# The values of an attention head, taken later inside the gate projection, with the low part of P last

## The chip, the cores and the metric

One NeuronCore of one Trainium2 chip. The metric is the device time of one execution in microseconds; lower is better. The kernel before takes 2942.22 us (median of 3 runs, 2941.56 to 2946.38).

## The reference, cut to what matters

Two layers of a decoder trunk on one sequence of 256 positions, width 2048, in f32. Each layer computes a normalised input `u`, one wide projection of it, an attention branch and a gated linear recurrence side by side, merges them with two sigmoid gates, and then runs an MLP and a per-layer embedding step.

```python
cq_raw, ckv_raw, xb, yb, gate_a, gate_r = split_columns(u @ w_in[l])
...
pr = jax.nn.softmax(sc, axis=-1).astype(v.dtype)
outs.append(jnp.einsum('bhqk,bkhd->bqhd', pr, v[:, :s1]))
...
merged = jax.nn.sigmoid(gate_a) * attn + jax.nn.sigmoid(gate_r) * rec
x = x + merged @ w_out[l]
```

The change is about the second line of the attention, probabilities (P) times values, for 16 heads with causal masking in two blocks of 128 queries.

## The kernel before, in words

**Arithmetic.** Every f32 operand of a matmul is split into a high and a low part (`hi` and `lo`, both of the type that TensorE takes), and a product is three matmuls: high by high, high by low, low by high (`mm3`, lines 214 to 219). ScalarE makes the high part (line 122 for weights, 964 for P), VectorE subtracts to get the low part (lines 126 and 967).

**Weights.** They arrive as blocks of 128 x 1024 ("halves" in the code, called blocks here), 1004 in all, by one DMA queue, into six raw buffers. `half()` (lines 202 to 212) starts the use of block h: it first splits block h + 2 (`split_half`, lines 117 to 128, three buffers each for `hi` and `lo`, so the new `hi` waits for the use of block h - 1 to end), and then lets the planner issue other work. `mm_half` (221 to 229) then issues the 24 matmuls of the block: 8 slices of 128 rows, three matmuls each, 256 columns wide.

**The planner.** The order of ScalarE's and VectorE's queues is written at build time by a small simulation. `E` holds a clock for each engine (P is TensorE); work is a list of jobs with steps, each step an engine, a cost and a function; jobs of lower rank come first. `later` adds a job, `need` makes TensorE's clock wait for one (and issues it if it was not yet), `work` issues the steps that start before a limit for each engine, those with no idle time first. `work` runs only inside `half()`: once between the `hi` and the `lo` of the split, with the limit for VectorE 0.18 below ScalarE's clock and none of ScalarE's own steps, and once after the split, with limits of P + 3.5 for VectorE and P + 2.6 for ScalarE. These are the lines that set it:

```python
        A.activation(hi, src, AF.Copy)
        E["A"] = max(E["A"], E["P"]) + 0.95
        work(E["A"] + LATENCY - 0.3, E["A"])
        V.tensor_tensor(out=lo, in0=src, in1=f(hi), op=ALU.subtract)
        E["V"] = max(E["V"], E["A"] + LATENCY) + 1.14
```

A product of one slice costs P 0.328, LATENCY is 0.12, and a step that follows another of its job starts 0.12 after it on another engine or the same.

**A group.** A layer's mixer runs 8 groups of two heads. For each group TensorE projects, in this order, the recurrence's input (`xb`, 4 blocks), its gelu branch (`yb`, 4), keys, values, queries and rope queries (1 each), the recurrence gate (`gr`, 4) and the attention gate (`ga`, 4); in group 0 `gr` comes ahead of the keys. Attention is threaded between those blocks by hooks, functions that `mm_pair` (line 250) and, for the last group's gate, `mm_apart` (line 261) call at the end of a block. In groups 1 to 7 the hooks of `gr` are `early` (line 992: scores of head 0 after block 2, of head 1 after block 3) and those of `ga` are `late`: after block 0 the transposes of head 0's P (`turned(0)`, line 955), after block 1 the values of head 0 and the transposes of head 1 (`values0`, 987), after block 2 the values of head 1 (`values(1)`, 971). In group 0 `early` sits in `ga`, and `late` in the `xb` blocks of group 1.

`turned` adds a job of rank -2 with two steps: the high part on ScalarE into `PT[0]` (line 964) and the low part on VectorE into `PT[1]` (line 967). `values` waits for it, takes the one bank of tag `o`, which must have been emptied of the head before (the copy `oT`, line 983, a job of rank -1), and issues six matmuls: for the first 128 keys, 256 columns (all queries), and then for the second 128 keys, 128 columns, each time high V by high P, high V by low P, low V by high P.

**The recurrence** is a job of rank 1 (line 906) whose last steps fall into the gate's blocks: `rec_b` (lines 894 to 896, planner cost 1.0), `rec_c`, a product and a scan (899 and 901, cost 1.3), `rec_d` (904, cost 0.6); then a job `recg` (782, cost 0.6).

Of the kernel before, what the change touches and what calls it, by code (L numbers as in the profile page):

```python
# [18 lines left out]
P = 128  # L19
S = 256  # L20
# [56 lines left out]
def trunk_kernel(ctx: ExitStack, tc: tile.TileContext, xT, pT, pos, par, gfin, invf, wu, out):  # L77
# [13 lines left out]
    V, A, T, G = nc.vector, nc.scalar, nc.tensor, nc.gpsimd  # L91

    def f(ap):
        return ap.bitcast(F32)
# [19 lines left out]
    E = {"P": 0.0, "V": 0.0, "A": 0.0, "G": 0.0}  # L114
# [55 lines left out]
    def later(key, *steps, deps=(), rank=1, also=()):  # L170

        job = Job((key, *also), rank, deps, steps)
        at = len(jobs)
        while at and jobs[at - 1].rank > rank:
            at -= 1
        jobs.insert(at, job)

    def need(key):

        if key not in done:  # L180
            next(j for j in jobs if key in j.keys).force()
        E["P"] = max(E["P"], done[key] + LATENCY)
# [19 lines left out]
    def half():  # L202
        h = nxt["used"]
        nxt["used"] += 1
        while nxt["half"] <= min(h + min(LA, max(h - 1, 0)), n_halves - 1):
            split_half(nxt["half"])
            nxt["half"] += 1
        load_to(h + PD)
        work(E["P"] + WINDOW + 0.9, E["P"] + WINDOW)
        hi, lo, at = halves.pop(h)  # L210
        E["P"] = max(E["P"], at)
        return hi, lo

    def mm3(o, wh, wl, ah, al, start, stop, shared=False):

        T.matmul(o, lhsT=wh, rhs=ah, start=start, stop=False, skip_group_check=shared)  # L216
        T.matmul(o, lhsT=wh, rhs=al, start=False, stop=False, skip_group_check=shared)  # L217
        T.matmul(o, lhsT=wl, rhs=ah, start=False, stop=stop, skip_group_check=shared)  # L218
        E["P"] += 0.328

    def mm_half(o, act, s, first=True, shared=False):


        hi, lo = half()
        for kk in range(8):
            k = 8 * s + kk
            need((act[1], k))
            c = slice(kk * P, (kk + 1) * P)
            mm3(o, hi[:, c], lo[:, c], act[0][:, k, 0, :], act[0][:, k, 1, :], first and k == 0, k == 15, shared)

    readers = {}

    def bank(tag, name, key):

        pool, bufs = banks[tag]
        last = readers.setdefault(tag, [])
        if len(last) >= bufs:
            need(last[-bufs])
        last.append(key)
        return pool.tile([P, 512], F32, tag=tag, name=name)  # L240

    def mm_bank(name, key):
        return bank("mm", name, key)

    def mm_tile(ps, act):

        for i in range(2):
            mm_half(ps[:, 0:S], act, i)

    def mm_pair(name, key, act, hooks=(), crossed=False):  # L250


        ps = mm_bank(name, key)
        for i in range(4):
            t, s = (i % 2, i // 2) if crossed else (i // 2, i % 2)
            mm_half(ps[:, t * S:(t + 1) * S], act, s, t == 0, True)
            if i < len(hooks) and hooks[i] is not None:
                hooks[i]()
        return ps

    def mm_apart(name, keys, act, hooks=()):

        for t in range(2):
            ps = mm_bank(f"{name}_{t}", keys[t])
            for s in range(2):
                mm_half(ps[:, 0:S], act, s)
                i = 2 * t + s
                if i < len(hooks) and hooks[i] is not None and s == 0:
                    hooks[i]()
            yield t, ps[:, 0:S]  # L270
            if i < len(hooks) and hooks[i] is not None:
                hooks[i]()

    def dup(r, n=2):
        return r.unsqueeze(1).to_broadcast([P, n, S])
# [4 lines left out]
    def t512(name):  # L280
        return tmp.tile([P, 512], F32, tag="t", name=name)
# [345 lines left out]
    def mixer(l, u, mg, norm):  # L627
# [73 lines left out]
        for g in range(GROUPS):  # L701
            first = group(l, g, u, mg, norm, cn, kr, first, rot_kr if g == 0 else None)

    def group(l, g, u, mg, norm, cn, kr, first, rot_kr):
# [3 lines left out]
        t_ = {}  # L708


        ps_x = mm_pair(f"xb_{nm}", ("xb", nm), u, first)

        def xb():
# [24 lines left out]


        ps_y = mm_pair(f"yb_{nm}", ("yb", nm), u)  # L740

        def y_evac():
# [62 lines left out]
        hi, lo = half()  # L805
        ps_v = mm_bank(f"v_{nm}", ("v", nm))
        for j in range(2):
            o = ps_v[:, j * S:(j + 1) * S]
# [49 lines left out]
        for t in range(2):  # L858
            ps_l = bank("s", f"lru{t}_{nm}", ("lru", t, nm))
            sl = slice(t * S, (t + 1) * S)  # L860
            for w in range(2):
                c = slice(512 + (2 * w + t) * P, 512 + (2 * w + t + 1) * P)
# [49 lines left out]
        def scores(t):  # L912
            for k in (("k", nm), ("q", nm), ("rot", f"q{nm}"), ("rot", f"k{l}")):
                need(k)
            s = bank("s", f"s{t}_{nm}", ("p", t, nm))
            for j in (1, 0):

                n = (j + 1) * P
                o = s[:, (1 - j) * S:(1 - j) * S + n]
                q = [t_["q"][w][:, t * S + j * P:t * S + (j + 1) * P] for w in "hl"]  # L920
                kk = [t_["k"][w][:, t * S:t * S + n] for w in "hl"]
                mm3(o, q[0], q[1], kk[0], kk[1], True, False)

                qr = t_["qr"]["q"][t][:, j * P:(j + 1) * P]
                for m, w in enumerate("hl"):
                    T.matmul(o, lhsT=qr, rhs=kr["rot"][w][:, 0:n], start=False, stop=m == 1)
                E["P"] += 0.22

            cols = (slice(0, S), slice(S, S + P))
            w = {}  # L930

            def mask_max():
                w["sm"] = t512(f"sm{t}_{nm}")
                w["st"] = tiny.tile([P, 8], F32, tag="st", name=f"st{t}_{nm}")
                for n, c in enumerate(cols):
                    V.tensor_tensor_reduce(
                        out=w["sm"][:, c], in0=s[:, c], in1=mask[:, n * P:S], scale=1.0, scalar=-3.0e38,
                        op0=ALU.add, op1=ALU.max, accum_out=w["st"][:, n:n + 1],
                    )
                V.tensor_scalar(out=w["st"][:, 2:4], in0=w["st"][:, 0:2], scalar1=-SCALE, scalar2=None, op0=ALU.mult)  # L940

            def expo():
                e = t_["p", t] = att.tile([P, 384], F32, tag=f"p{t}", name=f"p{t}_{nm}")
                for n, c in enumerate(cols):
                    A.activation(e[:, c], w["sm"][:, c], AF.Exp, bias=w["st"][:, 2 + n:3 + n], scale=SCALE, accum_out=w["st"][:, 4 + n:5 + n])

            def scale():
                V.reciprocal(w["st"][:, 6:8], w["st"][:, 4:6])
                e = t_["p", t]
                for n, c in enumerate(cols):  # L950
                    V.tensor_scalar(out=e[:, c], in0=e[:, c], scalar1=w["st"][:, 6 + n:7 + n], scalar2=None, op0=ALU.mult)

            later(("p", t, nm), ("V", 0.75, mask_max), ("A", 0.65, expo), ("V", 0.5, scale), rank=-1)

        def turned(t):
            need(("p", t, nm))
            e = t_["p", t]
            pt = bank("t", f"pt{t}_{nm}", ("pt", t, nm))
            T.transpose(pt[:, 256:384], e[:, 256:384], ident)
            T.transpose(pt[:, 384:512], e[:, 0:128], ident)  # L960
            T.transpose(pt[:, 128:256], e[:, 128:256], ident)

            def high():
                A.activation(PT[0][:, P:512], pt[:, P:512], AF.Copy)

            def low():
                V.tensor_tensor(out=PT[1][:, P:512], in0=pt[:, P:512], in1=f(PT[0][:, P:512]), op=ALU.subtract)

            later(("pt", t, nm), ("A", 0.4, high), ("V", 0.5, low), rank=-2)

        def values(t):
            need(("pt", t, nm))
            need(("v", nm))
            o = bank("o", f"o{t}_{nm}", ("o", t, nm))
            h, lo = PT
            for j, c in ((0, slice(S, 512)), (1, slice(P, S))):
                cc = slice(j * S + t * P, j * S + (t + 1) * P)
                mm3(o[:, j * P:S], t_["v"]["h"][:, cc], t_["v"]["l"][:, cc], h[:, c], lo[:, c], j == 0, j == 1)

            def evac():  # L980
                if t == 0:
                    t_["oT"] = att.tile([P, 512], F32, tag="oT", name=f"oT_{nm}")
                A.activation(t_["oT"][:, t * S:(t + 1) * S], o[:, 0:S], AF.Copy)

            later(("o", t, nm), ("A", 0.27, evac), rank=-1)

        def values0():
            values(0)
            turned(1)


        early, late = (None, None, lambda: scores(0), lambda: scores(1)), (lambda: turned(0), values0, lambda: values(1))
        if g:
            rec_gate(early)
        def merge_steps(t0, n):
# [21 lines left out]
        hooks = late if g else early  # L1017
# [349 lines left out]
```

## Time and profile before

| | |
|---|---|
| median of 3 runs | 2942.22 us |
| the profiled execution's own time | 2949.3 us |
| its span, first to last instruction | 2947.5 us |
| granted TensorE clock, mean | 0.998 |
| TensorE busy (matmuls) | 2907.9 us, 99% |
| VectorE busy | 1864.3 us, 63% |
| ScalarE busy | 1538.9 us, 52% |

TensorE executes 24800 matmuls, almost all of 128 x 128 by 256 columns. A matmul row is about 0.28 us long because it is pipelined; how fast TensorE goes is seen in the distance between starts. PE is TensorE, PEld its weight loads, DVE VectorE, ACT ScalarE. In a timeline a row gives the start, the duration, the engine, the line, the operation and the tiles (written from read), and in brackets the idle time of the engine just before it and what ended it.

### The profile page before, as it was taken

The page shows a single profiled execution, that of the slowest core. Times are in us where ns is not written, and L with a number is a line of the kernel's source. Part 1 is how long each engine was busy: PE and PEld are TensorE (multiplying, and loading weights), DVE is VectorE, ACT ScalarE, POOL GpSimd, SP SyncE. Part 2 cuts the span into 40 slices and gives each one's busy share as a digit, 9 for nine tenths or more (in the row PEclk, how much of TensorE's full clock was granted, in tenths as well). Part 3 has the DMA queues.
Part 4 walks back from the last instruction along what each step waited for, and adds up shares of the span by engine and source line. Part 5 has one row for each costly group of instructions (what it writes and reads, how often), then busy time and mean ns, then how long its engine had stood idle before and what let it go on. Part 6 is the DMA issues. An engine that isn't in the chain of part 4 may idle for free.

```text
span 2947.5 us, 58412 instructions
## 1 busy us (share of the span) xinstructions
PE 2907.9 (99%) x24800; PEld 2896.9 (98%) x24800; DVE 1864.3 (63%) x2420; ACT 1538.9 (52%) x2050; POOL 8.9 (0%) x17
## 2 busy tenths in 40 slices
PE   8999999999999999999999999999999999999998
PEld 8999999999999999999999999999999999999998
DVE  7877777765555454556758777776654555555565
ACT  5666666644344343444546666666543444434445
POOL 0000000000000000000000000000000000000000
PEclk9999999999999999999999999999999999999999
DMA  7555455555555555555555555555555555555553
GB/s 238 168 173 178 165 170 175 172 186 186 186 187 186 186 187 187 191 186 190 190 185 171 173 166 166 174 176 177 189 187 187 186 187 187 188 188 190 186 186 129
DMA packets 146998, 535.23 MB, mean 182 GB/s; under 512 B 16560, under 2 KB 16816, under 8 KB 146736
## 3 DMA queue, kind: packets, MB, share of 16 engines
q1 hardware_dynamic: 146736, 531.50, 54.9%
q8 instruction: 194, 3.18, 0.4%
q14 instruction: 68, 0.56, 0.0%
HBM read 529.33 MB, written 2.10 MB: 180 GB/s over the span
## 4 chain that ended last, share of the span: by engine, by line
PE 93%; DVE 3%; ACT 3%; issue 1%; DMA 0%; ACTq 0%; SPq 0%; POOLq 0%
PE down L218 8%; PE up L218 8%; PE down L217 8%; PE down L216 8%; PE up L216 8%; PE up L217 8%; PE yb L217 2%; PE gr L216 2%; PE yb L218 2%; PE yb L216 2%; PE out L217 2%; PE gr L218 2%; PE out L218 2%; PE gr L217 2%; PE out L216 2%; PE pg L217 2%
## 5 line engine op out<-in xcount | busy, mean ns | idle before, releaser
L126 DVE TENSOR_TENSOR lo<-raw,hi 128x1024 fp32r<-128x1024 f32 x1004 | 1229.8, 1225 | 878.5 <-ACT hi L122 876.3
L122 ACT ACTIVATE hi<-raw 128x1024 fp32r<-128x1024 f32 x1004 | 1066.0, 1062 | 1376.3 <-PE down L217 411.5
L216 PE MATMUL up<-bufA,hi 128*128 128x256 f32 x1024 | 287.9, 281 | 0.0
L216 PE MATMUL down<-bufB,hi 128*128 128x256 f32 x1024 | 287.7, 281 | 0.0
L217 PE MATMUL down<-bufB,hi 128*128 128x256 f32 x1024 | 287.7, 281 | 0.0
L218 PE MATMUL down<-bufB,lo 128*128 128x256 f32 x1024 | 287.7, 281 | 0.0
L216 PE MATMUL down<-bufA,hi 128*128 128x256 f32 x1024 | 287.7, 281 | 0.0
L217 PE MATMUL down<-bufA,hi 128*128 128x256 f32 x1024 | 287.7, 281 | 0.0
L218 PE MATMUL down<-bufA,lo 128*128 128x256 f32 x1024 | 287.7, 281 | 0.0
L216 PE MATMUL up<-bufB,hi 128*128 128x256 f32 x1024 | 287.7, 281 | 0.0
L217 PE MATMUL up<-bufA,hi 128*128 128x256 f32 x1024 | 287.6, 281 | 0.0
L218 PE MATMUL up<-bufA,lo 128*128 128x256 f32 x1024 | 287.6, 281 | 0.0
L218 PE MATMUL up<-bufB,lo 128*128 128x256 f32 x1024 | 287.5, 281 | 0.0
L217 PE MATMUL up<-bufB,hi 128*128 128x256 f32 x1024 | 287.5, 281 | 0.0
L217 PEld LDWEIGHTS down<-bufB,hi 128*128 128x128 f32 x1024 | 196.6, 192 | 0.0
L217 PEld LDWEIGHTS down<-bufA,hi 128*128 128x128 f32 x1024 | 196.6, 192 | 0.0
L217 PEld LDWEIGHTS up<-bufA,hi 128*128 128x128 f32 x1024 | 196.4, 192 | 0.0
L217 PEld LDWEIGHTS up<-bufB,hi 128*128 128x128 f32 x1024 | 196.4, 192 | 0.0
L216 PEld LDWEIGHTS up<-bufA,hi 128*128 128x128 f32 x1024 | 192.3, 188 | 0.0
L218 PEld LDWEIGHTS up<-bufB,lo 128*128 128x128 f32 x1024 | 192.2, 188 | 0.0
L218 PEld LDWEIGHTS up<-bufA,lo 128*128 128x128 f32 x1024 | 192.2, 188 | 0.0
L218 PEld LDWEIGHTS down<-bufB,lo 128*128 128x128 f32 x1024 | 192.2, 188 | 0.0
(551 smaller groups left out, 7857.8 us busy)
## 6 DMA issues: line engine op xcount, KB each, us to landing
raw<-wu SPq DMA_DIRECT2D x1004, 512.0 KB, 3.4
y<-rows SPq DMA_DIRECT2D x4, 512.0 KB, 4.0
x<-xT SPq DMA_DIRECT2D x3, 512.0 KB, 8.2
x<-xT SPq DMA_DIRECT2D x2, 256.0 KB, 4.3
praw<-pT SPq DMA_DIRECT2D x2, 256.0 KB, 4.6
parT<-par SPq DMA_DIRECT2D x1, 184.0 KB, 2.5
rope_w<-pos SPq DMA_DIRECT2D x1, 128.0 KB, 4.1
gf<-gfin SPq DMA_DIRECT2D x1, 8.0 KB, 8.1
```

The lines of the kernel that those rows point to most:

```text
L122: A.activation(hi, src, AF.Copy)
L126: V.tensor_tensor(out=lo, in0=src, in1=f(hi), op=ALU.subtract)
L216: T.matmul(o, lhsT=wh, rhs=ah, start=start, stop=False, skip_group_check=shared)
L217: T.matmul(o, lhsT=wh, rhs=al, start=False, stop=False, skip_group_check=shared)
L218: T.matmul(o, lhsT=wl, rhs=ah, start=False, stop=stop, skip_group_check=shared)
```

## The change

The hooks of a block may now be a pair: the first of the two runs after the fourth of the block's eight slices, the second at the end. `values0` moves from the end of block 1 of the gate to the middle of block 2, and with it the transposes of head 1; `values(1)` moves from the end of block 2 to the middle of block 3. `turned(0)` stays. The six matmuls of `values` are the same six, in another order: the four with the high part of P, then the two with the low part. The planner is told 0.6 for them instead of 2 x 0.328.

```diff
+    def mm_half(o, act, s, first=True, shared=False, mid=None):
...
             mm3(o, hi[:, c], lo[:, c], act[0][:, k, 0, :], act[0][:, k, 1, :], first and k == 0, k == 15, shared)
+            if kk == 3 and mid is not None:
+                mid()
...
         for i in range(4):
             t, s = (i % 2, i // 2) if crossed else (i // 2, i % 2)
-            mm_half(ps[:, t * S:(t + 1) * S], act, s, t == 0, True)
-            if i < len(hooks) and hooks[i] is not None:
-                hooks[i]()
+            mid, end = hook_of(hooks, i)
+            mm_half(ps[:, t * S:(t + 1) * S], act, s, t == 0, True, mid)
+            end()
...
+    def hook_of(hooks, i):
+        h = hooks[i] if i < len(hooks) else None
+        mid, end = h if isinstance(h, tuple) else (None, h)
+        return mid, end or (lambda: None)
...
             h, lo = PT
-            for j, c in ((0, slice(S, 512)), (1, slice(P, S))):
-                cc = slice(j * S + t * P, j * S + (t + 1) * P)
-                mm3(o[:, j * P:S], t_["v"]["h"][:, cc], t_["v"]["l"][:, cc], h[:, c], lo[:, c], j == 0, j == 1)
+            vh, vl = (t_["v"][w] for w in "hl")
+            ops = [(v, h, j) for j in range(2) for v in (vh, vl)] + [(vh, lo, j) for j in range(2)]
+            for n, (v, q, j) in enumerate(ops):
+                c = slice(P, S) if j else slice(S, 512)
+                T.matmul(
+                    o[:, j * P:S], lhsT=v[:, j * S + t * P:j * S + (t + 1) * P], rhs=q[:, c], start=n == 0, stop=n == 5,
+                    skip_group_check=True,
+                )
+            E["P"] += 0.6
...
-        early, late = (None, None, lambda: scores(0), lambda: scores(1)), (lambda: turned(0), values0, lambda: values(1))
+        early, late = (None, None, lambda: scores(0), lambda: scores(1)), (lambda: turned(0), None, (values0, None), (lambda: values(1), None))
```

`mm_apart`, for the last group, takes the same pairs.

## Rows read from the trace of the kernel before

**Rows 1.** The page: busy time by engine, and the chain that ended last, by engine.

```profile
PE 2907.9 (99%) x24800; PEld 2896.9 (98%) x24800; DVE 1864.3 (63%) x2420; ACT 1538.9 (52%) x2050; POOL 8.9 (0%) x17
...
PE 93%; DVE 3%; ACT 3%; issue 1%; DMA 0%; ACTq 0%; SPq 0%; POOLq 0%
```

**Rows 2.** Waits: engine, line, waited for: total us, times, longest.

```profile
PEld o L217 <- DVE pt_lo L967: 21.5, 30, 1.2
...
PE o L217 <- DVE pt_lo L967: 15.4, 28, 1.0
...
PE pt L959 <- DVE p L951: 1.7, 2, 0.9
```

**Rows 3.** Timeline of TensorE, gate blocks 1 to 3 of group 1, layer 0.

```profile
177.00 0.37 PE L216 MATMUL ga<-bufA,hi 128*128 128x256 f32 x1
...
179.82 0.28 PE L216 MATMUL o<-pt_hi,v_1h 128*128 128x256 f32 x1
180.55 0.39 PE L217 MATMUL o<-pt_lo,v_1h 128*128 128x256 f32 x1 [0.45 <-DVE pt_lo L967]
...
181.17 0.30 PE L959 MATMUL pt<-ident,p 128*128 128x128 f32 x1
...
181.44 0.36 PE L216 MATMUL ga<-bufA,hi 128*128 128x256 f32 x1
...
184.36 0.28 PE L216 MATMUL o<-pt_hi,v_1h 128*128 128x256 f32 x1
185.18 0.39 PE L217 MATMUL o<-pt_lo,v_1h 128*128 128x256 f32 x1 [0.55 <-DVE pt_lo L967]
...
185.81 0.33 PE L216 MATMUL ga<-bufA,hi 128*128 128x256 f32 x1
...
188.68 0.28 PE L216 MATMUL xb<-bufA,hi 128*128 128x256 f32 x1
```

**Rows 4.** Timeline of VectorE, the same stretch.

```profile
179.95 0.55 DVE L967 TENSOR_TENSOR pt_lo<-pt,pt_hi 128x384 fp32r<-128x384 f32 x1
180.41 0.42 DVE L894 TENSOR_SCALAR ee<-ee 128x512 f32<-128x512 f32 x1
...
181.59 0.69 DVE L899 TENSOR_TENSOR thx<-thx,zz 128x512 f32<-128x512 f32 x1
182.32 1.23 DVE L901 TENSOR_TENSOR_SCAN hh<-ee,thx 128x512 f32<-128x512 f32 x1
183.46 1.20 DVE L126 TENSOR_TENSOR lo<-raw,hi 128x1024 fp32r<-128x1024 f32 x1
184.58 0.55 DVE L967 TENSOR_TENSOR pt_lo<-pt,pt_hi 128x384 fp32r<-128x384 f32 x1
185.04 0.68 DVE L904 TENSOR_TENSOR hh<-hh,y 128x512 f32<-128x512 f32 x1
```

**Rows 5.** Timeline of ScalarE, the same stretch.

```profile
181.00 1.04 ACT L122 ACTIVATE hi<-raw 128x1024 fp32r<-128x1024 f32 x1
181.95 0.47 ACT L964 ACTIVATE pt_hi<-pt 128x384 fp32r<-128x384 f32 x1
182.32 0.38 ACT L983 ACTIVATE oT<-o 128x256 f32<-128x256 f32 x1
184.44 1.06 ACT L122 ACTIVATE hi<-raw 128x1024 fp32r<-128x1024 f32 x1 [1.74 <-PE ga L217]
```

**Rows 6.** Timelines of VectorE and TensorE, groups 0 and 7 of layer 0.

```profile
134.17 0.55 DVE L967 TENSOR_TENSOR pt_lo<-pt,pt_hi 128x384 fp32r<-128x384 f32 x1
...
138.19 0.28 PE L216 MATMUL yb<-bufA,hi 128*128 128x256 f32 x1
...
549.55 0.55 DVE L967 TENSOR_TENSOR pt_lo<-pt,pt_hi 128x384 fp32r<-128x384 f32 x1
...
554.52 0.55 DVE L967 TENSOR_TENSOR pt_lo<-pt,pt_hi 128x384 fp32r<-128x384 f32 x1
```

**Rows 7.** A stretch of group 7: busy PE, PEld, DVE, ACT, POOL; granted clock; DMA.

```profile
545.00:560.00 15.00, 13.59 (x114) 13.04 (x114) 12.70 (x25) 10.28 (x18) 0.00 (x0) 1.00 0.41 132
```

More of the change, by code (lines that the diff above doesn't have):

```diff
@@ L219, in mm3 @@
         E["P"] += 0.328
-    def mm_half(o, act, s, first=True, shared=False):
+    def mm_half(o, act, s, first=True, shared=False, mid=None):
         hi, lo = half()
@@ L265, in mm_apart @@
             for s in range(2):
[L266 to L269, printed above, removed]
+                mid, end = hook_of(hooks, 2 * t + s)
+                mm_half(ps[:, 0:S], act, s, mid=mid)
+                if s == 0:
+                    end()
             yield t, ps[:, 0:S]
-            if i < len(hooks) and hooks[i] is not None:
-                hooks[i]()
+            end()
     def dup(r, n=2):
```

## The prediction

> **What bounds the kernel now.** I read the page first. TensorE is busy for 99% of the span and carries 93% of the chain that ended last [rows 1]: time is lost only where TensorE stands still. The list of waits says where: nearly all of it is one place, the values of a head, whose second matmul waits for the low part of P from VectorE, 28 times, 15.4 us of idle matmul, 21.5 us counted at the weight loads; two further waits, 1.7 us, stand before a transpose [rows 2]. There are 32 calls of values (2 layers, 8 groups, 2 heads). The rest is the timeline of one group, group 1 of layer 0 [rows 3 to 5]; the other thirteen groups from 1 to 7 in the two layers show the same picture.
>
> There the gate block 1 runs from 177.00 to 179.82; values(0) starts at 179.82, waits at its second matmul until 180.55, a loss of 0.6 us; the transposes of head 1 follow at 181.17, block 2 runs from 181.44 to 184.36, values(1) waits until 185.18, 0.7 us more; block 3 runs from 185.81 and the next group begins at 188.68 [rows 3]. In each case TensorE resumes 0.05 us after pt_lo ends (180.50 and 185.13 [rows 4]). VectorE is the late one: between the two pt_lo it works without a gap (L894 to L901 of the recurrence, 1.91 us from 181.59 to the next start for the product and the scan, then one 1.20 us lo) [rows 4].
>
> **The change, part by part.**
>
> *Values(0) half a block later.* 12 matmuls at (179.82 - 177.00) / 24 = 0.117 us are 1.41 us. It would start at 181.23, and pt_lo is ready at 180.50 [rows 3, 4]. Its loss goes: two thirds of a microsecond per group. The first group of each layer has no such loss, but its transpose wait (1.7 us for two [rows 2]) is covered by the same 1.4 us.
>
> *Low part last.* The first use of pt_lo moves from second matmul to fifth, three matmuls later, about 0.3 us. The number of matmuls, weight loads and their widths is unchanged: cost zero, and no DMA is added or moved; the weight queue only sees its raw buffers freed by a lo a little later, with six in turn.
>
> *Values(1) and the transposes half a block later.* This is where the order of VectorE changes, and the term that decides. The transposes' copies are queued only when the planner runs, at the start of a block, and there the split of a coming half goes first: hi, then what fits into the window that ends 0.18 us before the planner's A, then lo, then everything else. Before, the transposes stood ahead of block 2, so pt_lo(1) went behind the lo split there. Now they stand inside block 2, so pt_lo(1) goes behind the lo split at block 3, one lo more, while values(1) waits for it only half a block into block 3.
>
> Where the recurrence goes I took from the planner's own costs, which give an order and no time. I worked its books through up to block 1 of the gate, and count from P there: V stands at 1.03 and A at 1.22. Block 1: A = 1.22 + 0.95 = 2.17, lo to 2.17 + 0.12 + 1.14 = 3.43, pt_hi(0) to 2.57, pt_lo(0) to 3.93, the tanh of the recurrence gate to 3.09, P = 8 x 0.328 = 2.62. At block 2: A = 3.09 + 0.95 = 4.04, the V window ends at 3.86, below V, so L894 to L896 (cost 1.0) do not get in ahead of lo as they did; lo ends at 5.30; the second window reaches 6.12, so they go behind it, to 6.30, and the product and scan (1.3), ready at 6.42, do not. P: 3.94 in the middle, 4.05 for pt_lo(0), 4.65 behind values(0), 5.96 at block 3. There A = 6.91, the window ends at 6.73, 6.42 fits: product and scan go ahead of lo, and pt_lo(1) behind both. So VectorE's order becomes pt_lo(0), lo, L894 to L896, product and scan, lo, pt_lo(1).
>
> With durations of the trace: hi of block 2 ends at 182.04 as before, for ScalarE's queue up to it is unchanged [rows 5], and VectorE, which worked at 180.41 before, now stands idle until it. lo 182.09 to 183.3; L894 to the product 1.18 (180.41 to 181.59), to 184.4; product and scan 1.96 (181.59 to 183.55), to 186.4; lo 1.20, of which 0.1 overlaps, to 187.5; pt_lo 0.55, again with 0.1 overlapped, to 187.97 [rows 4]. Its other inputs are earlier: block 2 ends near 183.6, hi takes 1.06 from 183.7, pt_hi 0.47 and oT 0.38 behind it to about 185.4, which values(1) needs for its one bank [rows 5]. So values(1) starts its high part at 185.4 instead of 185.0, and its fifth matmul at 188.02 instead of 185.4: a stall of 2.6 us where the two of before made 1.3 to 1.5. Behind that matmul TensorE's queue holds the last 12 matmuls of the gate and the whole next block; the gate's evacuation and the release of the hi buffer move with them.
>
> Against before: pt_lo(1) ends 187.97 - 185.13 = 2.84 us later. The work behind its first use was 3.50 us (185.18 to 188.68 [rows 3]), and is now two value matmuls, 0.22, and 12 gate matmuls, 1.41: 1.63, so 1.87 less. **+0.97 us per group**; bounds 0.7 and 1.2 (block 2 took 0.1 us more than block 1 for the same 24 matmuls, so each interruption of a block is worth 0.1 either way, and there are two). Twelve groups (1 to 6, two layers): **+11.6 us**. The planner's P at the next group's first block is the same as before, so I let each group begin with the same queues.
>
> The Trainium skill (TensorE: Matmul & The Clock Gate, "Back-to-back issue gap") gives 262 cycles for 256 columns at full clock, 0.109 us, below the spacing of this trace. By it the 12 matmuls would take 1.31 us and the sum would be 1.2 us smaller; the row is used.
>
> *Last group of a layer (two).* The small evacuation of its first gate tile takes VectorE's place behind lo at block 2, so product and scan are ready at 6.80 by the same books and miss the window (6.73): they go behind pt_lo(1). In group 1's times pt_lo(1) would end at 184.73 + 1.2 + 0.45 = 186.40, and this group runs 369.60 us later (549.55 against 179.95, the first pt_lo; its second one ended at 555.07 [rows 6]): 556.0, 1.0 later, less 1.87: -0.87 each, **-1.7 us**. Bounds -1.9 and 0. The merge that follows it is due in the third half of the next block row, some 7 us later, so it stays covered.
>
> *First group of a layer (two).* lo, then L904 and L782 (0.68 and about as much [rows 4]), lo, pt_lo: it ends near 137.2 instead of 134.72, 2.5 later; the work behind was 138.19 - 134.77 = 3.42 and becomes 1.63 [rows 6]: +0.7 each, **+1.4 us**; bounds 0 and 1.5, since one of these steps fits by only 0.06 in the books.
>
> Sum: 11.6 - 1.7 + 1.4 = **+11.3 us**. The profiled execution took 2949.3 us (span 2947.5); it becomes 2960.6. The median of the three runs, 2942.22, lies 7.1 us lower; I add the same 11.3: **2953.5 us**. A measurement of this kernel tells about 0.2%, 5.9 us, from no change.
>
> **Rivals.**
> *A. The recurrence stays behind pt_lo(1) in all groups.* It decides if the product is ready later than the window's end, and the margin is 0.31 in planner units. Then pt_lo(1) ends at 186.40, 1.57 earlier than forecast, and 0.97 becomes -0.60: 12 x -0.60 - 1.7 + 1.4 = -7.5 us, **2934.7**, faster. For it: the last group does just that. Against: the books above, the same in all twelve groups.
> *B. Both waits vanish, as the shift suggests at first sight.* 21.5 us at the weight loads and 1.7 for the transposes [rows 2]: -23 us, **2919**. Against: the distance from the transposes of head 1 to its values stays one block, and gains only three matmuls, while pt_lo(1) gets one more lo ahead of it.
> *C. The two shifts cancel* (values(0) saves what values(1) adds): **2942**.
> *D. The longer stop costs clock.* One idle of about 2 us stands where two of 0.45 and 0.55 did. The granted clock is 1.00 over a stretch in which TensorE idles 1.4 of 15 us [rows 7]; were the 36 matmuls after each stop at 1.2 instead of 2.4 GHz, they would take 4.2 us more: +50 us, **about 3004**.
>
> **How the numbers follow.** Forecast 0.74, A 0.12, B 0.06, C 0.04, D 0.04. The forecast's own range is 2947 to 2960 (terms at their bounds: 6.5 to 15.9 us, taken 2 us wider). The range for 8 in 10 must reach into A, the nearest case on the other side: 2933 to 2960; B and D stay out. Slower: the forecast less the few hundredths of it below 5.9 us, and D, 0.74; faster: A and most of B, 0.16; the rest 0.10.
>
> **What would show it.** In the list of waits, values on pt_lo should fall from 28 waits to about 16, each near 2 us, and total near 30 us; the values of head 0 should not wait at all, and the transposes neither. In VectorE's timeline of a middle group there should be an idle of 1.5 us before the lo of block 2, and between the two pt_lo the order lo, L894, product, scan, lo. If the scan stands behind the second pt_lo, rival A holds and the total of these waits is below before; if waits of values(1) are under 0.5 us, the whole reading of the queue is wrong.

## The result, and the profile after

The changed kernel is slower: 2972.59 us (median of 4 runs, 2968.78 to 2974.91) against 2944.24 of the kernel before (4 runs), a ratio of 1.0095 with an interval from 1.0078 to 1.0113. That is 28 us where 11.3 were forecast, and above the range, which ended at 2960. The profiled execution's span is 2972.2 us against 2947.5, 24.7 longer. The two differences are not the same because the profiled execution of the kernel before, 2949.3 us, was slower than its four timed runs (2941.56 to 2946.38).

The list of TensorE's waits, in the columns of [rows 2]:

```profile
PE o L989 <- DVE pt_lo L975: 24.8, 14, 1.9
...
PE o L989 <- ACT oT L998: 6.6, 16, 0.7
```

Sixteen calls of `values` wait instead of 28, but longer: 24.8 and 6.6, 31.4 us in all, where [rows 2] had 15.4 and 1.7. The transposes no longer wait. (Lines behind the edit have moved: 975 was 967, 989 stands for the six matmuls of `values`, 902 to 909 were 894 to 901.)

VectorE in group 1 of layer 0, the stretch of [rows 4]:

```profile
182.07 0.55 DVE L975 TENSOR_TENSOR pt_lo<-pt,pt_hi 128x384 fp32r<-128x384 f32 x1
184.20 1.23 DVE L126 TENSOR_TENSOR lo<-raw,hi 128x1024 fp32r<-128x1024 f32 x1 [1.58 <-ACT hi L122]
185.34 0.42 DVE L902 TENSOR_SCALAR ee<-ee 128x512 f32<-128x512 f32 x1
...
186.52 0.69 DVE L907 TENSOR_TENSOR thx<-thx,zz 128x512 f32<-128x512 f32 x1
187.25 1.22 DVE L909 TENSOR_TENSOR_SCAN hh<-ee,thx 128x512 f32<-128x512 f32 x1
188.39 1.20 DVE L126 TENSOR_TENSOR lo<-raw,hi 128x1024 fp32r<-128x1024 f32 x1
189.51 0.55 DVE L975 TENSOR_TENSOR pt_lo<-pt,pt_hi 128x384 fp32r<-128x384 f32 x1
```

The order is the forecast one: lo, L902 (the L894 of before), product, scan, lo, pt_lo, with an idle of 1.58 us ahead of the first lo. From the first pt_lo to the second it takes 7.44 us, where it took 4.63 [rows 4].

TensorE in the same group, beside [rows 3]:

```profile
183.31 0.28 PE L989 MATMUL o<-pt_hi,v_1h 128*128 128x256 f32 x1
...
184.21 0.37 PE L216 MATMUL ga<-bufA,hi 128*128 128x256 f32 x1
...
187.57 0.39 PE L989 MATMUL o<-pt_hi,v_1h 128*128 128x256 f32 x1 [0.38 <-ACT oT L998]
...
190.11 0.44 PE L989 MATMUL o<-pt_lo,v_1h 128*128 128x256 f32 x2 [1.87 <-DVE pt_lo L975]
...
191.83 0.28 PE L216 MATMUL xb<-bufA,hi 128*128 128x256 f32 x1
```

Values(0) runs through without a wait; values(1) waits twice, first for its bank, then 1.87 us for pt_lo. From the first pt_lo to the next group's first block it is 9.76 us (182.07 to 191.83), before 8.73 (179.95 to 188.68): 1.03 more, where 0.97 was forecast.

So far this is the forecast. What its sum did not contain is in the granted clock, the speed at which the chip lets TensorE run, as a share of the full one. Seven stretches of 3.4 us, and one ordinary stretch for comparison (columns: start and end, length, busy time of PE and its matmuls, granted clock, DMA share, GB/s):

```profile
138.20:141.60 3.40, 3.40 (x18) 0.50 0.27 106
315.70:319.10 3.40, 3.40 (x18) 0.50 0.36 136
380.60:384.00 3.40, 3.40 (x18) 0.51 0.35 130
506.90:510.30 3.40, 3.40 (x19) 0.51 0.32 124
1725.40:1728.80 3.40, 3.40 (x18) 0.50 0.21 78
1851.70:1855.10 3.40, 3.40 (x19) 0.50 0.34 133
1916.60:1920.00 3.40, 3.40 (x19) 0.51 0.19 74
320.00:323.40 3.40, 3.40 (x31) 1.00 0.42 154
```

Each follows a stop of values(1), and in each TensorE is busy all the time but runs 18 or 19 matmuls instead of 31: it runs at 1.2 GHz instead of 2.4. What one such fall costs shows in the distance between the same place of two groups that follow each other, the first matmul of values(0):

```profile
183.31 0.28 PE L989 MATMUL o<-pt_hi,v_1h 128*128 128x256 f32 x1
...
245.71 0.28 PE L989 MATMUL o<-pt_hi,v_2h 128*128 128x256 f32 x1
...
372.89 0.28 PE L989 MATMUL o<-pt_hi,v_4h 128*128 128x256 f32 x1
...
436.88 0.28 PE L989 MATMUL o<-pt_hi,v_5h 128*128 128x256 f32 x1
```

From group 1 to 2 there is no fall and it is 62.40 us; from group 4 to 5, with the fall at 380.60 and the blocks otherwise at the same pace, it is 63.99: 1.6 us. Seven times, that is 11.2 us. (In two of the groups it is 2.4 us, because the blocks behind the fall also ran at the slower of the two paces of the last section.) In the kernel before there is no such stretch between the start and the end of the run. It is not one execution's luck: all four runs have a mean granted clock of 0.995, where the profile of before has 0.998.

### The profile page after: what moved, and what is told of

It reads as the page before. It is cut to its first block, busy times and chain, and to the rows that moved or that the text cites. A ratio compares the mean times of both kernels' runs of the same rounds, so it can differ in the third digit from the quotient of the medians.

```text
span 2972.2 us, 58396 instructions
## 1 busy us (share of the span) xinstructions
PE 2918.2 (98%) x24800; PEld 2908.0 (98%) x24800; DVE 1864.2 (63%) x2420; ACT 1534.7 (52%) x2050; POOL 8.9 (0%) x17
## 4 chain that ended last, share of the span: by engine, by line
PE 94%; DVE 2%; ACT 1%; issue 1%; DMA 0%; SPq 0%; ACTq 0%; POOLq 0%
PE down L218 8%; PE up L218 8%; PE down L216 8%; PE down L217 8%; PE up L216 8%; PE up L217 8%; PE gr L216 2%; PE out L218 2%; PE out L217 2%; PE out L216 2%; PE gr L217 2%; PE gr L218 2%; PE yb L216 2%; PE yb L218 2%; PE yb L217 2%; PE xb L216 2%
## 5 line engine op out<-in xcount | busy, mean ns | idle before, releaser
L217 PEld LDWEIGHTS up<-bufB,hi 128*128 128x128 f32 x1024 | 196.4, 192 | 0.0
L216 PEld LDWEIGHTS up<-bufB,hi 128*128 128x128 f32 x1024 | 192.3, 188 | 0.0
```

## The experiments

Each ratio is to runs of the kernel before on the same chip: 2944.06 us for the runs with four fillers, with the scan behind, and with the remedy at the ends of the blocks; 2949.51 for the other four. A stop, below, is what a call of `values` takes beyond one that waits for nothing; that takes 0.76 us, from the start of the last matmul ahead of the six to the start of the first behind them.

**The new order of the six matmuls alone.** The edit to the kernel before is the body of `values`:

```diff
-            for j, c in ((0, slice(S, 512)), (1, slice(P, S))):
...
+            ops = [(v, h, j) for j in range(2) for v in (vh, vl)] + [(vh, lo, j) for j in range(2)]
...
```

> The kernel before, with the six matmuls of the values in the new order alone (the two with the low part of P last), the hooks where they were. Theory (VectorE sets the end of both stops): pt_lo of head 1 ends when it did, so only the three matmuls that now stand ahead of the wait of head 1 are saved, 0.35 us in each of 16 groups, since what is saved at head 0 is waited for at head 1: 5 us under before, 2939. Rival (each wait is a loss of its own): 0.35 us at 30 waits, 10 us, 2934. The granted clock stays at 1.00 in both.

Measured 2937.62 us, ratio 0.9963 (0.9948 to 0.9977): 11 us faster.

```profile
PE o L980 <- DVE pt_lo L967: 8.6, 16, 0.7
```

The number is the rival's, the mechanism mostly the theory's. In the timelines of groups 1 to 6 the wait of head 0 is 0.35 us shorter and that of head 1 as long as before (a stop of 0.8 to 0.9 us): one saving per group, as expected, 14 x 0.35 = 4.9 us. But in the last group of each layer the wait of head 1 is gone, 1.2 us each: there the planner, told 0.6 instead of 0.656, put the product and scan behind pt_lo. With that 7.3 us; the rest, some 4 us in the profile, came from the pace of ordinary blocks (last section).

**The hooks in the middle alone**, the changed kernel with the old order of the six:

```diff
-            ops = [(v, h, j) for j in range(2) for v in (vh, vl)] + [(vh, lo, j) for j in range(2)]
...
+            for j, c in ((0, slice(S, 512)), (1, slice(P, S))):
...
```

> The changed kernel with the values in the old order (low part of P second), so the hooks in the middle of the blocks alone. Theory (the place of the hooks is the whole loss): the stop of head 1 in groups 1 to 6 begins three matmuls earlier and ends when it did, so 0.35 us more behind it in each group, 5 us over the changed kernel, and its longest idle grows from 1.9 to about 2.2 us; with as many or more falls of the granted clock to 0.50 (seven of 1.6 us now): 2977 to 2988. Rival (the new order itself costs time, for example by alternating widths): below the changed kernel, under 2970.

Measured 2976.17 us, ratio 1.0095 (1.0077 to 1.0113), by time not to be told from the whole change, and just under the theory's 2977. The trace is clearer:

```profile
PE o L217 <- DVE pt_lo L975: 29.0, 16, 2.1
...
PE o L216 <- ACT oT L992: 6.6, 16, 0.7
```

35.6 us of waits instead of 31.4, nine stretches at half clock instead of seven (one of them twice as long), and a span of 2981.7. So the hooks alone bring the whole loss. Beside the longer stop the gain of the order shows in the waits, 4 us, but not beyond the intervals in time; the two falls of the clock fewer in this pair of profiles may be chance.

**Filling the long wait.**

```diff
+FILL = 12
...
+                if n == 4 and t == 1:
+                    for _ in range(FILL):
+                        T.matmul(
+                            o[:, S:512], lhsT=vh[:, t * P:(t + 1) * P], rhs=h[:, S:512], start=False, stop=False,
+                            skip_group_check=True,
+                        )
```

> The changed kernel with 12 more matmuls of 256 columns in each values of head 1, between the four with the high part and the two with the low part, into the unused half of their bank: the output is not touched. They take 1.3 us of a wait of 1.87 and change nothing that VectorE does. Theory (a part of the loss is the granted clock, which falls to 0.50 after the long idle): no stretch at 0.50 in the middle of the run, 11 us less, plus some 1.5 us where the wait is shorter than the filler (group 7): about 2963. Rival (those stretches cost nothing that the waits do not already cost): 2972 to 2976, with the stops of 2.8 us per group as they are.

Measured 2958.07 us, ratio 1.0032 (1.0021 to 1.0042): with 192 matmuls more than the changed kernel it is 0.6%, some 18 us, faster. The stretch that ran at half clock in the changed kernel, here:

```profile
315.70:319.10 3.40, 3.40 (x33) 1.00 0.08 27
```

There is no stretch at 0.50 between start and end of this run, and the long waits are left at 4.0 us:

```profile
PE o L996 <- ACT oT L1005: 6.4, 16, 0.7
PE o L996 <- DVE pt_lo L976: 4.0, 12, 0.4
```

VectorE's order is the same, so the stop lasts as long; only TensorE is busy in it. Profile against profile the span is 17.1 us shorter (2955.1 against 2972.2). Seven falls at 1.6 us are 11.2 of these, and 6.8 are a faster pace of the output projection in both layers (last section); 2.1 are lost again in the last group of each layer, where the fillers take longer than the wait, and the small rest is the pace of other blocks. So the clock accounts for some 11 of the 18 us; that the faster pace comes from the fillers is not shown.

**Four fillers instead of twelve.** `FILL` is 4 in the edit above.

> The changed kernel with 4 filler matmuls instead of 12 in the wait of head 1, so an idle of about 1.4 us in groups 1 to 6 where it was 1.87. Theory (the length of the idle decides whether the granted clock falls): fewer stretches at 0.50 than seven, as the 1.2 us idles of group 0 had one in two. Rival (any idle there makes it fall): seven or so again. Time 2962 to 2972.

One run: 2973.19 us, 29 over the kernel before on that chip, and six stretches at half clock, behind idles of 1.2 to 1.4 us:

```profile
PE o L996 <- DVE pt_lo L976: 17.1, 14, 1.4
```

The time is that of the changed kernel, a little above the 2972 expected. With 7.7 us less idle the falls are six instead of seven, and in groups 1 to 6 of the two layers six of twelve stops are followed by one in both kernels: as far as one run tells, the rival holds there. In group 0, where the fillers leave idles of 0.7 us, there is none. A wait of 1.2 to 1.4 us, with the shorter one for the bank ahead of it, was enough for the fall in some groups.

**P's copies ahead of the next split**, the changed kernel with

```diff
             values(0)
             turned(1)
+            for key in (("pt", 1, nm), ("o", 0, nm)):
+                next(j for j in jobs if key in j.keys).force()
```

> The changed kernel, with the copies of head 1's transposed P (high and low) and the evacuation of head 0's values issued at once behind the transposes, ahead of the split of the next block on ScalarE and VectorE. Theory (the order of VectorE is the cause): pt_lo of head 1 ends near 184.9 in the times of before, when its values come: nearly all waits for pt_lo vanish, no fall of the granted clock, 23 us under before, about 2921. Rival (the shift of the hooks delays something else, such as the one bank of the values or the recurrence): at or above before, 2944 or more.

Measured 2927.01 us, ratio 0.9927 (0.991 to 0.9943): 21.5 us faster than before, some 49 faster than the changed kernel (0.9927 against 1.0095), and no wait of `values` is left in its list. VectorE in group 1:

```profile
181.86 0.42 DVE L902 TENSOR_SCALAR ee<-ee 128x512 f32<-128x512 f32 x1
182.33 0.69 DVE L904 SCALAR_TENSOR_TENSOR thx<-thx,xc 128x512 f32<-128x512 f32 x1
...
182.93 0.55 DVE L975 TENSOR_TENSOR pt_lo<-pt,pt_hi 128x384 fp32r<-128x384 f32 x1
183.40 1.21 DVE L126 TENSOR_TENSOR lo<-raw,hi 128x1024 fp32r<-128x1024 f32 x1
184.53 0.68 DVE L907 TENSOR_TENSOR thx<-thx,zz 128x512 f32<-128x512 f32 x1
```

pt_lo ends at 183.48, 4.34 us after the end of the one before it (179.14), and the lo and the product follow it. No instruction was added or taken away on any engine; three steps, the two copies and the evacuation of head 0's values, went ahead of others.

**Product and scan behind pt_lo** (rival A), one planner cost in the changed kernel:

```diff
-            ("rec", nm), ("V", 1.3, rec_a), ("A", 1.8, rec_s), ("V", 1.0, rec_b), ("V", 1.3, rec_c), ("V", 0.6, rec_d),
+            ("rec", nm), ("V", 1.3, rec_a), ("A", 1.8, rec_s), ("V", 1.4, rec_b), ("V", 1.3, rec_c), ("V", 0.6, rec_d),
```

> The changed kernel with one planner cost altered: 1.4 instead of 1.0 for the recurrence step ahead of the product and scan, so that these miss the window at block 3 of the gate and go behind pt_lo of head 1 in every group. No instruction is added or taken. This is rival A of the prediction. Theory: pt_lo of head 1 ends 1.57 us earlier in groups 1 to 6, the stop is near 1.2 us with an idle of 0.4, no fall of the granted clock: 19 us and 11 us under the changed kernel, some 7 under before, about 2940 where before is 2947. Rival (the additional split ahead of pt_lo matters, the scan does not): no more than 5 us under the changed kernel.

Measured 2940.33 us, ratio 0.9989 (0.998 to 0.9999), 3 us under before and some 31 under the changed kernel. Product and scan now follow pt_lo in groups 1 to 7:

```profile
185.32 1.22 DVE L126 TENSOR_TENSOR lo<-raw,hi 128x1024 fp32r<-128x1024 f32 x1 [0.42 <-ACT hi L122]
186.47 0.55 DVE L975 TENSOR_TENSOR pt_lo<-pt,pt_hi 128x384 fp32r<-128x384 f32 x1
186.93 0.68 DVE L907 TENSOR_TENSOR thx<-thx,zz 128x512 f32<-128x512 f32 x1
```

```profile
PE o L989 <- DVE pt_lo L975: 7.8, 14, 1.4
...
PE o L989 <- ACT oT L998: 6.3, 16, 0.6
```

The stop of 2.7 us became 1.3, and no stretch at half clock is left. The price of 7.5 us that the prediction gave rival A was about twice too high: the first group of a layer lost more (its waits make 2.3 us instead of the 1.2 of before, 1.1 more where 0.7 was forecast; its recurrence was put elsewhere), and a middle group gained 0.33 instead of 0.60 (from its first pt_lo to the next group's first block 8.37 us, where it was 8.71, means of the twelve groups).

**The same remedy with the hooks at the ends**, now for the copies of both heads: the kernel before, the new order of the six, and in `turned`

```diff
             later(("pt", t, nm), ("A", 0.4, high), ("V", 0.5, low), rank=-2)
+            for key in (("pt", t, nm), ("o", 0, nm))[:1 + t]:
+                next(j for j in jobs if key in j.keys).force()
```

> The kernel before with the new order of the six matmuls, the hooks at the ends of the blocks as before, and the copies of the transposed P of both heads (and the evacuation of head 0's values) issued at once behind the transposes, ahead of the next split. Theory (the order on ScalarE and VectorE decides, not the place of the hooks): pt_lo is ready one block after its transposes, no wait for it, the same as the version with the hooks in the middle: 22 us under before, about 2925 where before is 2947. Rival (the half block is needed as well): waits for pt_lo remain and it stays 5 us or more above that version.

Measured 2927.18 us, ratio 0.9942 (0.9928 to 0.9957), 17 us under before where 22 were expected, and the same as the version with the hooks in the middle within their intervals. `values` waits nowhere; the transposes in the first group of each layer wait for the softmax, as in the kernel before and somewhat longer:

```profile
PE pt L959 <- DVE p L951: 2.6, 2, 1.3
```

So the half block is not what is needed: with P's copies ahead of the split, the place of the hooks is worth these 2.6 us, which the version with the hooks in the middle does not wait, and nothing more is to be seen (spans 2924.1 and 2921.3).

## Why the prediction was right or wrong

**What bounds the kernel, and the order of the queue: right.** TensorE lost time only at the values; values(0) and the transposes stopped waiting; the order on VectorE came out step for step, idle included, and pt_lo came 7.44 us after its predecessor, forecast 187.97 - 180.50 = 7.47. (One reading was off: from the product to the start of the lo behind the scan it is 1.87 us in [rows 4], 181.59 to 183.46, not 1.91; the sum does not use it.) The runs with P's copies ahead and with the scan behind show that this order is the cause and not only a companion: both remove the loss by order alone.

**The middle groups: the size was right at full clock.** In the six of these groups without a fall of the clock it takes 9.74 to 9.76 us from the first pt_lo to the next group's first block, where the same groups took 8.64 to 8.74: 1.0 to 1.1 more each, forecast 0.97, and some 12.5 us for twelve groups, forecast 11.6.

**First and last groups: right.** The last group's two stops make 1.3 us instead of 1.9, so it gains 0.7 (forecast 0.87). The first group of a layer stops for 2.1 us instead of 1.2; the blocks of `xb` that hold its values take 15.10 us instead of 14.40 in layer 1, where no fall lies in them, so it loses 0.7 (forecast 0.7).

**The step that failed: the clock, put at nothing in the sum (rival D).** The prediction put the clock aside with the row in which TensorE idles 1.4 of 15 us at a granted clock of 1.00 [rows 7]. That row holds two short waits, 0.44 and 0.97 us, several us apart, and says nothing of one of 1.87 with another close ahead of it. The mechanism was named, with its place, and given 4 in 100; the price was taken as 36 matmuls at half speed in all twelve middle groups, 4.2 us each and 50 in all, where it is 1.6 us in seven stops of sixteen, 11.2 us. The forecast's own terms came to some 12.5 us as measured; with 11.2 that is 23.7, against 24.7 between the two profiles. The sum should have carried the clock as a term of its own, bounded between nothing and every stop; so carried, the range would have held the result.

**What is left of the 24.7 us** is about 1, and it is a balance of paces: the output projection of layer 1 ran at the slower of two paces in the profile of the changed kernel and at the faster one before (768 matmuls at 0.0045 us difference, 3.4 us), and against it more of the `xb` and `yb` stages ran at the faster one. That either belongs to the change is not shown; the paces come and go between kernels.

**Rivals B and C** fell with the order of the queue: nearly all of B's 23 us was there to be had (21.5 measured), but only by putting P's copies ahead, which the change does not do. C's two shifts do not cancel: what values(0) saves is less than what values(1) adds.

## What to carry to other kernels

Where a planner issues work only at certain points, moving a producer off such a point can put it behind a whole further batch; ask for a moved step not only how much later its consumer comes, but at which of these points it now enters each queue. One long stop of TensorE can be dearer than two short ones, since the granted clock may fall after it: here the two waits of 0.4 to 1.0 us per group were never followed by a fall, the single one of 1.87 us in six groups of twelve. Price it as a term. Where the order can't be mended, matmuls that change nothing can be worth their work if they fill nearly all of the wait; twelve were, four were not. And when a wait is for one small step behind a large one, try first to put the small one ahead: here that gained 17 to 21 us, and the longer distance alone lost 28.

## What the runs showed of the hardware that was not expected

**The granted clock fell after idles of 1.2 to 2.1 us, but not after each.** It did so at seven of the sixteen calls of values(1) in the changed kernel (idles of 1.87 and 1.2 us), at nine in the one with the hooks alone (2.0 to 2.1 and 1.5), at six with four fillers (1.2 to 1.4), at none where the twelve fillers left at most 0.7 us, and at none with the scan behind, where most stops were 1.3 us in two waits of 0.6 us or less, though the two first groups had idles of 1.4 us there. Nor did it fall after the two idles of 1.3 us ahead of the transposes in the run with the remedy at the ends of the blocks. Why one idle of the same length is followed by a fall and the next is not stays open.

**Ordinary blocks run at one of two paces, at the same granted clock.** A stretch of the output projection of layer 1 before, and one of the changed kernel (columns as above):

```profile
2030.00:2060.00 30.00, 30.00 (x267) 1.00 0.59 196
```

```profile
2050.00:2080.00 30.00, 30.00 (x257) 1.00 0.58 186
```

267 matmuls against 257 in 30 us, all of 256 columns: 24 of them take 2.72 or 2.83 us, and a run of blocks mostly keeps its pace over a whole stage. The MLP went at the slower one in each profile, but for a few of its first blocks; the output projection at either, in both layers at the faster in the runs with P's copies ahead (but for a few blocks) and with twelve fillers. What decides which of the two a stage gets was not tried; at 0.1 us per block it is worth 7 us over the two output projections alone, and it moves the medians by some us between kernels whose waits are the same. The Trainium skill (TensorE: Matmul & The Clock Gate, "Back-to-back issue gap") gives 262 cycles as the isolated gap for 256 columns, 0.109 us at full clock; both paces here, 0.113 and 0.118, lie above it, and the measured ones decide.
